# Reordering the written schedule of an attention stage: value tiles by halves of rows, normalisation next to its sums, pool weights loaded early

## The chip, the cores and the metric

The kernel runs on one core of a Trainium2 chip. The metric is device time in microseconds (us) of one execution; the median of several runs is compared. Each run of a comparison is made on the same chip as the kernel it is compared with.

## The reference: what is computed

One layer of an encoder trunk over 1024 tokens of width 1024, all in float32:

```python
hn = rmsnorm(h, norm_mix_g[i])
z = hn @ w_in[i]                       # 512 pool columns, then q, k, v of 8 heads x 64
a = pool_mixer(u, pool_w[i], ...)      # 4 groups, trailing windows 2, 4, 8, 16
o = chunk_attention(q, k, v, rel_bias[i])  # chunk of 64 attends to itself and 8 chunks before
h = h + jnp.concatenate([a, o], axis=-1) @ w_out[i]
# then a gated MLP with a causal convolution and GELU, a sigmoid gate with a
# per-layer input, and a last rmsnorm
```

The softmax is over the band of 576 positions with a relative-position bias for each head. The change touches the attention stage and the first half of the output projection behind it; the MLP and the gate, which take the last 830 us or so, stay as they are.

## The kernel before

**Products.** Every float32 product is made of three matmuls: each operand is split into a high part (rounded, written by ScalarE with a copy) and a low part (the rest, written by VectorE with a subtraction). The helper `mm3` (lines 117 to 119) issues high x high, high x low and low x high into one PSUM bank. `split` (lines 122 and 123) makes the two parts.

**The attention stage** works on pairs of heads (4 pairs) and, inside a pair, on tiles of 128 queries (8 tiles). A *unit* is one pair and one query tile; tiles 0 and 1 share a unit, so there are 7 units in a pair (`PER`) and 28 in all (`NU`). `unit(u)` writes the instructions of a unit in this order:

1. `probs_t(u - 1)`: TensorE transposes the probabilities of the unit before (line 407) into PSUM banks 2 and 3, and what has no room there into banks 6 and 7. `probs_out` brings them to SBUF as high part (ScalarE, line 426) and low part (VectorE, line 427).
2. `scores(u)`: TensorE makes the scores of the unit (line 383) in banks 4 to 7.
3. `softmax`: VectorE adds the bias and takes the extreme of each row (lines 351 and 355), ScalarE takes the exponential and its sum (line 363), VectorE takes the reciprocal (line 365), and the rows are scaled by it: those of the first head of the pair by VectorE (line 361), those of the second by ScalarE (line 359).
4. *Fill*: TensorE works on the projection of what later units need: q and k of the next pairs, the second half of the values, then the pool columns. The generators `project` and `project_v` yield after each step: one block of 128 rows of the contraction (three matmuls of 512 columns) in `project`, two blocks (six matmuls of 256 columns) in `project_v`. A unit is allowed a number of steps (`ROOM`, 5.5 to 7), and a running `credit` carries over what was taken too much or too little.
5. `values(u - 1)`: after every second query tile, TensorE multiplies values and probabilities (lines 451 and 452). Before it, while the unit is not the last and the state variable `at[0]` is below 1.6, more fill steps are taken, and each is charged to `credit`. `at[0]` says how far the current accumulation has come: it keeps the product away from the first moments of an accumulation, since it uses the PSUM bank that the projection is not in.

The projections alternate between PSUM banks 0 and 1 (`bankn`). A finished half is read out of its bank by `qk_out` (VectorE, line 263), by `v_outs` (ScalarE 254, VectorE 255) or for the pool columns by line 549. `lay` makes the high and low parts of q and k (lines 292 to 296). Weights are split by `split_later` (lines 475 and 472) into one of two ring slots (`wring`); the two row halves of the value weights (`wv2[0]`, `wv2[1]`) lie in the same two slots.

**The order** on TensorE, ScalarE and VectorE in this stage is written out, not planned: TensorE takes its instructions as the program issues them, and for the other two `push(due, ...)` files each instruction under a due time inside its unit, and `flush()` issues what is filed in the order of these due times. So the numbers in `push` set the order on both engines. Waits between engines follow from what is read and written; two engines are never let into the same PSUM bank at once, and the later one in program order waits. Outside this stage a planner orders all engines but TensorE, and it may bring later instructions into idle places of the stage.

**Behind the stage** come the pool mixer and the output projection. `tail` holds the running sums of the two narrow pool groups (VectorE, lines 564 to 580), which use a piece of the buffer `F` from 57.5 KB on as scratch; the two wide groups run on GpSimd (`later`). `out_mm(d, ...)` accumulates one block of output rows (12 matmuls), and `mix(g)` between them multiplies one pool group by its weights in banks 6 and 7 and reads it out with line 594. The pool weights are loaded and split in the first call of `mix`, into ring slot 1, which the last projection of the stage uses until its end.

Of the kernel before, what the change touches and what calls it, by code (L numbers as in the profile page):

```python
# [11 lines left out]
P = 128  # L12
# [70 lines left out]
def trunk(tc, xT, pT, vecs, w_qk0, w_in, w_v, bias, counts, pool_w, w_out, w_up, w_down,  # L83
# [4 lines left out]
    with tc.tile_pool(name="sb", bufs=1) as sb, \  # L88
# [20 lines left out]
        def f(kb, n):  # L109
            return F[:, int(kb * KW):int(kb * KW) + n]  # L110

        def rv(ap):
            return ap.bitcast(F32)

        def mm3(ps, ahi, alo, bhi, blo, first, last, more=False):

            pe.matmul(ps, ahi, bhi, start=first, stop=False, skip_group_check=more)  # L117
            pe.matmul(ps, ahi, blo, start=False, stop=False, skip_group_check=more)  # L118
            pe.matmul(ps, alo, bhi, start=False, stop=last, skip_group_check=more)  # L119

        def split(src, hi, lo, pinned=False):
            both = (act.activation(hi, src, AF.Copy),  # L122
                    dve.tensor_tensor(lo, src, rv(hi), ALU.subtract))  # L123
            if pinned:
                for i in both:
                    tc.keep_in_program_order(i)
# [122 lines left out]
        def v_outs(t, half, ps):  # L249
            s = rstd_tok[:, t:t + 1]  # L250
            pv = ps.rearrange("p (h c) -> p h c", h=4)
            hs = slice(4 * half, 4 * half + 4)
            hi, lo = V[:, t, hs, 0:HD], V[:, t, hs, HD:2 * HD]
            return (lambda: act.activation(hi, pv, AF.Copy, scale=s),
                    lambda: dve.scalar_tensor_tensor(lo, pv, s, rv(hi), ALU.mult, ALU.subtract))
# [5 lines left out]
        def qk_out(c, h, ps):  # L261
            hs = slice(h * 512, (h + 1) * 512)
            dve.tensor_tensor(qk32[c][:, hs], ps, rstd_bc[:, hs], ALU.mult)
# [4 lines left out]
        def push(t, *fns):  # L268

            for n, fn in enumerate(fns):  # L270
                pending.append((t + 0.8 * n, len(pending), fn))

        def flush():
            todo = sorted(pending, key=lambda p: p[:2])
            pending.clear()
            owed.clear()
            for _, _, fn in todo:
                fn()
# [65 lines left out]
        def softmax(todo):  # L344

            for i, (x, b, ps, S, s_) in enumerate(todo):
                z = 2 * i / len(todo)

                def least(b=b, ps=ps, S=S, s_=s_):
                    if len(ps.shape) == 3:  # L350
                        dve.tensor_tensor_reduce(  # L351
                            S.rearrange("p (a b) -> p a b", a=2), ps,
                            b.rearrange("p (a b) -> p a b", a=2), 1.0, BIG, ALU.add, ALU.min, s_[:, 0:1])
                    else:
                        dve.tensor_tensor_reduce(S, ps, b, 1.0, BIG, ALU.add, ALU.min, s_[:, 0:1])

                def scaled(x=x, S=S, s_=s_):
                    if x:
                        act.activation(S, S, AF.Copy, scale=s_[:, 2:3])  # L359
                    else:  # L360
                        dve.tensor_scalar(S, S, s_[:, 2:3], None, ALU.mult)
                push(1.0 + 0.8 * z, least)
                push(1.9 + 0.85 * z, lambda S=S, s_=s_: act.activation(  # L363
                    S, S, AF.Exp, bias=s_[:, 0:1], scale=-1.0, accum_out=s_[:, 1:2]))
                push(3.4 + 0.35 * z, lambda s_=s_: dve.reciprocal(s_[:, 2:3], s_[:, 1:2]))
                push(3.9 + 0.1 * z, scaled)

        halves = [slice(HD * x, HD * x + HD) for x in range(2)]

# [51 lines left out]
        def probs_out(todo):  # L421
            n = 0
            for x, q, a, b, bank, ps in todo:
                src = ps.rearrange("p a (k q) -> p a k q", q=HD)
                hi, lo = [PT[x][:, y, a:b, q:q + P].rearrange("p k (a q) -> p a k q", a=2) for y in range(2)]
                push(0.9 if bank > 3 else 0.3 * n, lambda hi=hi, src=src: act.activation(hi, src, AF.Copy))  # L426
                push(2.6 + 0.3 * n, lambda lo=lo, src=src, hi=hi: dve.tensor_tensor(lo, src, rv(hi), ALU.subtract))  # L427
                n += bank < 4

        credit, turns = 0.0, []  # L430
# [35 lines left out]

        def split_later(ct, parts, soon=False):

            t = now[0] if soon else max(5.2, now[0] + 0.4)
            for i, (src, hi, lo) in enumerate(parts):  # L470
                def low(src=src, hi=hi, lo=lo, end=i == len(parts) - 1):
                    dve.tensor_tensor(lo, src, rv(hi), ALU.subtract)
                    if end:
                        there.add(ct)
                push(t + 0.7 * i, lambda src=src, hi=hi: act.activation(hi, src, AF.Copy), low)

        def v_weights(z):
            split_later(("v", z), [(wvr[z][:, k], wv2[z][0][:, k], wv2[z][1][:, k])
# [38 lines left out]
        def project_v():  # L517
            v_weights(1)
            flush()
            for t in range(NTOK):  # L520
                bankn[0] += 1
                bank = bankn[0] % 2
                if bank in owed:
                    flush()
                for k in range(KT):
                    if (t, k) == (NTOK - 1, 4):
                        weights(8 + 3)
                    mm3(PS[:, bank, 0:256], XTH[t // 4][:, k, t % 4 * P:(t % 4 + 1) * P],
                        XTL[t // 4][:, k, t % 4 * P:(t % 4 + 1) * P], wv2[k // 4][0][:, k % 4], wv2[k // 4][1][:, k % 4],
                        k == 0, k == KT - 1)  # L530
                    if k % 2:
                        at[0] = 0.36 * (k + 1)
                        yield True
                push(now[0] + 0.2, *v_outs(t, 1, PS[:, bank, 0:256]))
                owed.add(bank)
                v_ready.append(t)

        def project_qk(p):

            for x in (1, 0):  # L540
                def evac(h, ps, x=x):
                    push(now[0] + 0.2, lambda: qk_out(x, h, ps))
                    qk_ready.append((p, x, h))
                yield from project(4 + 4 * x + p, evac, (p - 1, (x,)))

# [34 lines left out]
                eng.scalar_tensor_tensor(u[:, f0:n], src[:, f0:n], 1.0 / win, u[:, f0:n], ALU.mult, ALU.subtract)  # L580

        def mix(g):
            if g == 2:
                t = load(pool_w, 512)
                split(t, pwh, pwl)
            yh, yl = ya[g % 2]
            a32 = a32s[g % 2]
            split(U[:, g, HIST:], yh, yl)
            for h in range(2):
                hs = slice(h * 512, (h + 1) * 512)  # L590
                ps = PS[:, 6 + h]
                gs = slice(g * P, (g + 1) * P)
                mm3(ps, pwh[:, gs], pwl[:, gs], yh[:, hs], yl[:, hs], True, True)
                act.activation(a32[:, hs], ps, AF.Identity, bias=pbs[:, g:g + 1],
                               scale=vec[:, C_PS + g:C_PS + g + 1])
                split(a32[:, hs], catp[h][:, g, 0], catp[h][:, g, 1])
# [39 lines left out]
        def lay_due(u):  # L636

            for c, x, h in list(qk_ready):
                if u >= (c - 1) * PER + (0 if x else PER - 1 if h else 2):
                    qk_ready.remove((c, x, h))  # L640
                    push(max(5.2, now[0] + 0.4), *lay(c, x, h))

        for h in range(3):
            load_bias(h)()
# [39 lines left out]

        weights(8 + 1)
        flush()
        with tc.manual_schedule(engines={mybir.EngineType.Activation, mybir.EngineType.DVE}):
            for u in range(NU + 1):
                unit(u)
        for _ in fill:  # L690
            flush()
        flush()
        run_later(len(later))
        for fn in tail:
            fn()
# [59 lines left out]
        first_b = (2, 3, 4, 5, 0, 1, 6, 7)  # L755
        for z, d in enumerate(first_d):
            out_mm(d, 0, first_b[z], attn, True, False)
            if 1 <= z <= 4:
                mix((2, 3, 0, 1)[z - 1])
        for d in first_d:  # L760
            sp.dma_start(H[d], xT[d])
        out_weights(1, pooled)
# [670 lines left out]
```

## Time and profile before

| what | us |
|---|---|
| median of 3 runs | 1139.28 (1137.82 to 1139.57) |
| the profiled execution | 1138.94, span 1137.2 |
| TensorE busy | 1119.2 (98% of the span) |
| VectorE, ScalarE, GpSimd busy | 863.7, 588.7, 144.3 |
| mean granted TensorE clock | 0.996 of full speed |
| attention stage | from about 54 to 271 us |
| output projection, first half | from about 282 to 338 us |

Times in the profile count from the first instruction. A matmul's end is modelled, so starts are more reliable than durations. A group line shows an instruction's source line, engine, operation, what it writes and reads, the shapes, the count, busy time and mean, then the idle time of the engine just before and who ended it. A list of waits says who waited for whom, how long in total, how often, and the longest. A timeline row shows start, duration and instruction, and in brackets the idle time before it.

### The profile page before, as it was taken

Reading aid. Unit: us, or ns where it says so; the run is one execution under the profiler, and the core shown is the slowest. Engines: PE = TensorE matmul, PEld = TensorE weight load, DVE = VectorE, ACT = ScalarE, POOL = GpSimd, SP = SyncE. Lnnn points to the kernel's source line nnn. Section 1 sums busy time; section 2 is a strip of 40 time slices with the busy share of each in tenths; the row PEclk is TensorE's granted clock in tenths of the full one; section 3 lists DMA queues with packets and bytes.
Section 4 is the critical chain, followed back from the end, with each engine's and each line's share of the span. In section 5 each row is a group of like instructions: output and inputs, shape, how many; then the busy total and the mean of one; then the engine's idle time right before and its main releaser. Section 6 shows DMA issues by size and latency. Waiting matters only on the chain.

```text
span 1137.2 us, 16199 instructions
## 1 busy us (share of the span) xinstructions
PE 1119.2 (98%) x5914; PEld 936.4 (82%) x5914; DVE 863.7 (76%) x1508; ACT 588.7 (52%) x1052; POOL 144.3 (13%) x188
## 2 busy tenths in 40 slices
PE   9999999999999999999999999999999999999997
PEld 7988787888788888888888887888888888888887
DVE  8577657678758888887787878777878789986845
ACT  8376667665654554444444444444444445564634
POOL 0000000065002200120112011211021102000000
PEclk9999999999999999999999999999999999999999
DMA  7111101105500154575557655765576555520003
GB/s 279 38 37 43 38 24 37 50 23 183 194 13 16 48 150 146 135 178 142 132 155 158 164 133 150 157 162 142 149 153 157 153 149 115 164 93 19 1 30 118
DMA packets 64879, 125.91 MB, mean 111 GB/s; under 512 B 7328, under 2 KB 8736, under 8 KB 64800
## 3 DMA queue, kind: packets, MB, share of 16 engines
q1 hardware_dynamic: 50688, 99.38, 26.8%
q0 software_dynamic: 13824, 25.17, 14.0%
q8 instruction: 46, 0.75, 0.3%
q10 hardware_dynamic: 288, 0.33, 0.1%
q14 instruction: 33, 0.27, 0.1%
HBM read 110.18 MB, written 14.68 MB: 110 GB/s over the span
## 4 chain that ended last, share of the span: by engine, by line
PE 88%; DVE 6%; ACT 3%; issue 2%; DMA 1%; POOL 0%; SPq 0%; POOLq 0%; DVEq 0%; ACTq 0%
PE PS L117 28%; PE PS L118 27%; PE PS L119 27%; DVE B L427 2%; DVE F L351 2%; PE PS L451 1%; PE PS L452 1%; ACT B L426 1%; PE PS L383 1%; PE PS L407 1%; ACT F L454 1%; DVE R L123 0%; PE PS L739 0%; DMA F<-in_xT 0%; ACT F L359 0%
## 5 line engine op out<-in xcount | busy, mean ns | idle before, releaser
L117 PE MATMUL PS<-R 128*128 128x512 f32 (+1 forms) x1104 | 425.6, 386 | 1.7 <-ACT F L909 0.8
L118 PE MATMUL PS<-R 128*128 128x512 f32 (+1 forms) x1104 | 422.4, 383 | 0.2 <-DVE R L228 0.2
L119 PE MATMUL PS<-R 128*128 128x512 f32 (+1 forms) x1104 | 421.9, 382 | 0.0
L117 PEld LDWEIGHTS PS<-R 128*128 128x128 f32 x1104 | 208.2, 189 | 45.1 <-issue 2.1
L118 PEld LDWEIGHTS PS<-R 128*128 128x128 f32 x1104 | 208.2, 189 | 40.2 <-DVE R L228 1.5
L119 PEld LDWEIGHTS PS<-R 128*128 128x128 f32 x1104 | 207.9, 188 | 40.5
L122 ACT ACTIVATE R<-F 128x512 fp32r<-128x512 f32 (+2 forms) x221 | 138.1, 638 | 175.2 <-PE PS L118 80.2
L123 DVE TENSOR_TENSOR R<-F,R 128x512 fp32r<-128x512 f32 (+2 forms) x221 | 152.8, 703 | 37.3 <-ACT R L122 35.9
L822 DVE TENSOR_TENSOR F<-F 128x512 f32<-128x512 f32 x88 | 61.5, 699 | 49.0 <-DMA F<-in_w_up 45.7
L1132 DVE TENSOR_TENSOR F<-F,PS 128x512 f32<-128x512 f32 x140 | 92.3, 680 | 6.2 <-PE PS L119 6.0
L122 ACT ACTIVATE BQ<-RW 128x512 fp32r<-128x512 f32 x90 | 52.6, 622 | 77.1 <-PE PS L118 73.1
L1075 POOL DMA_DIRECT2D RW<-Yd x56 | 49.4, 883 | 262.6 <-DMA RW<-Yd 201.0
L1075 POOL DMA_DIRECT2D RW<-in_w_down x40 | 36.1, 946 | 233.8 <-DMA RW<-in_w_down 193.0
L123 DVE TENSOR_TENSOR BQ<-RW,BQ 128x512 fp32r<-128x512 f32 x90 | 59.0, 683 | 2.1 <-PE PS L118 1.3
L118 PE MATMUL PS<-BQ 128*128 128x512 f32 x140 | 54.6, 390 | 0.1
L119 PE MATMUL PS<-BQ 128*128 128x512 f32 x140 | 54.5, 389 | 0.0
L118 PE MATMUL PS<-R,BQ 128*128 128x512 f32 x140 | 54.5, 389 | 0.0
L117 PE MATMUL PS<-BQ 128*128 128x512 f32 x140 | 54.5, 389 | 0.0
L117 PE MATMUL PS<-R,BQ 128*128 128x512 f32 x140 | 54.5, 389 | 0.0
L119 PE MATMUL PS<-R,BQ 128*128 128x512 f32 x140 | 54.5, 389 | 0.0
L958 ACT ACTIVATE F<-F,vec 128x1024 f32<-128x1024 f32 (+1 forms) x25 | 28.6, 1143 | 48.6 <-DVE F L933 42.9
L363 ACT ACTIVATE F<-F,small 128x640 f32<-128x640 f32 (+4 forms) x64 | 44.0, 691 | 16.7 <-DVE small L351 15.0
(179 smaller groups left out, 1704.6 us busy)
## 6 DMA issues: line engine op xcount, KB each, us to landing
F<-in_w_up SPq DMA_DIRECT2D x91, 256.0 KB, 4.3
RW<-Yd SPq DMA_DIRECT2D x60, 256.0 KB, 3.6
RW<-Yd POOLq DMA_DIRECT2D x56, 256.0 KB, 5.0
RW<-in_w_down SPq DMA_DIRECT2D x50, 256.0 KB, 2.8
RW<-in_w_down POOLq DMA_DIRECT2D x40, 256.0 KB, 6.3
Yd<-F SPq DMA_DIRECT2D x40, 256.0 KB, 3.8
F<-in_w_in SPq DMA_DIRECT2D x10, 512.0 KB, 3.5
F<-in_xT SPq DMA_DIRECT2D x16, 256.0 KB, 5.8
```

The source lines that it names most:

```text
L117: pe.matmul(ps, ahi, bhi, start=first, stop=False, skip_group_check=more)
L118: pe.matmul(ps, ahi, blo, start=False, stop=False, skip_group_check=more)
L119: pe.matmul(ps, alo, bhi, start=False, stop=last, skip_group_check=more)
L122: both = (act.activation(hi, src, AF.Copy), dve.tensor_tensor(lo, src, rv(hi), ALU.subtract))
L123: dve.tensor_tensor(lo, src, rv(hi), ALU.subtract))
L351: dve.tensor_tensor_reduce(S.rearrange("p (a b) -> p a b", a=2), ps, b.rearrange("p (a b) -> p a b", a=2), 1.0, BIG, ALU.add, ALU.min, s_[ ...
L363: push(1.9 + 0.85 * z, lambda S=S, s_=s_: act.activation(S, S, AF.Exp, bias=s_[:, 0:1], scale=-1.0, accum_out=s_[:, 1:2]))
L427: push(2.6 + 0.3 * n, lambda lo=lo, src=src, hi=hi: dve.tensor_tensor(lo, src, rv(hi), ALU.subtract))
L822: return dve.tensor_tensor(rawu[to], rawu[a], rawu[b], op)
L958: act.activation(y, Gb[:, 2 + a:2 + b], AF.Identity, bias=vec[:, C_CB + fi:C_CB + fi + 1], scale=cw(2))
L1075: pool.dma_start(t, src, accum_op=ALU.add)
L1132: dve.tensor_tensor(t, t, PS[:, 4 + d], ALU.subtract if n in (1, 5) else ALU.add)
```

## The change

Five things change, all in the order of work.

- **Softmax order.** The reciprocals are due earlier (2.95 and 3.5 instead of 3.4 and 3.75), and the scaling on VectorE is due right behind its reciprocal (3.0 instead of 3.9). The copy of the transposed probabilities out of banks 6 and 7 is due at 3.6 instead of 0.9; the subtractions for all pieces but the first are due at 3.55 to 4.4 instead of 2.9 to 3.5.
- **Reading out.** `qk_out` and `v_outs` are due 0.2 earlier, the second instruction of `v_outs` 0.5 instead of 0.8 after the first; `lay` is due from 4.8 instead of 5.2.
- **Value tiles.** For the first two tiles (0 and 1) and the last two (6 and 7) the first four row blocks of both tiles are done first, then the last four of both, so two accumulations are open at once. While such a pair is open `at[0]` is 0.0, and it rises to 0.72 and 1.44 in the last half of the second tile. The split of the second half of the value weights is due before the rest (`now - 0.3`). The weights of the next projection are asked for before the second half of tile 6 instead of in the middle of tile 7.
- **Pool weights** are loaded in unit 23 into the buffer `F` at 57.5 KB, and split right behind the stage, ahead of `tail`.
- **The mixer** starts after the third block of the output projection instead of the second.

```diff
-                push(3.4 + 0.35 * z, lambda s_=s_: dve.reciprocal(s_[:, 2:3], s_[:, 1:2]))
-                push(3.9 + 0.1 * z, scaled)
+                push(2.95 + 0.55 * z, lambda s_=s_: dve.reciprocal(s_[:, 2:3], s_[:, 1:2]))
+                push(3.9 + 0.1 * z if x else 3.0 + 0.55 * z, scaled)
...
-                push(0.9 if bank > 3 else 0.3 * n, lambda hi=hi, src=src: act.activation(hi, src, AF.Copy))
-                push(2.6 + 0.3 * n, lambda lo=lo, src=src, hi=hi: dve.tensor_tensor(lo, src, rv(hi), ALU.subtract))
+                push(3.6 if bank > 3 else 0.3 * n, lambda hi=hi, src=src: act.activation(hi, src, AF.Copy))
+                push(4.4 if bank > 3 else 3.55 + 0.05 * n if n else 2.6, lambda lo=lo, src=src, hi=hi: dve.tensor_tensor(lo, src, rv(hi), ALU.subtract))
...
-            t = now[0] if soon else max(5.2, now[0] + 0.4)
+            t = now[0] - 0.3 if soon else max(5.2, now[0] + 0.4)
...
-                push(t + 0.7 * i, lambda src=src, hi=hi: act.activation(hi, src, AF.Copy), low)
+                push(t + 0.7 * i * (not soon), lambda src=src, hi=hi: act.activation(hi, src, AF.Copy))
+                push(t + (0.25 + 0.02 * i if soon else 0.8 + 0.7 * i), low)
...
-            for t in range(NTOK):
-                bankn[0] += 1
-                bank = bankn[0] % 2
-                if bank in owed:
-                    flush()
-                for k in range(KT):
-                    if (t, k) == (NTOK - 1, 4):
-                        weights(8 + 3)
...
+            order = [(t, z) for t in range(NTOK) for z in range(2)]
+            order[1:3] = order[2:0:-1]
+            order[-3:-1] = order[-2:-4:-1]
+            banks = {}
+            for t, z in order:
+                if z == 0:
+                    bankn[0] += 1
+                    banks[t] = bankn[0] % 2
+                    if banks[t] in owed:
+                        flush()
+                ps = PS[:, banks[t], 0:256]
+                paired = t in (0, 1, NTOK - 2, NTOK - 1)
+                if (t, z) == (NTOK - 2, 1):
+                    weights(8 + 3)
+                for k in range(4 * z, 4 * z + 4):
...
                     if k % 2:
-                        at[0] = 0.36 * (k + 1)
+                        at[0] = 0.36 * (k + 1) if not paired else 0.36 * (k - 3) if z and t % 2 else 0.0
                         yield True
-                push(now[0] + 0.2, *v_outs(t, 1, PS[:, bank, 0:256]))
-                owed.add(bank)
-                v_ready.append(t)
+                if z:
+                    hi, lo = v_outs(t, 1, ps)
+                    push(now[0], hi)
+                    push(now[0] + 0.5, lo)
+                    owed.add(banks[t])
+                    v_ready.append(t)
...
-                    push(now[0] + 0.2, lambda: qk_out(x, h, ps))
+                    push(now[0], lambda: qk_out(x, h, ps))
...
-            if g == 2:
-                t = load(pool_w, 512)
-                split(t, pwh, pwl)
...
-                    push(max(5.2, now[0] + 0.4), *lay(c, x, h))
+                    push(max(4.8, now[0] + 0.4), *lay(c, x, h))
...
+        pw = f(57.5, 512)
         with tc.manual_schedule(engines={mybir.EngineType.Activation, mybir.EngineType.DVE}):
             for u in range(NU + 1):
                 unit(u)
+                if u == NU - PER + 2:
+                    sp.dma_start(pw, pool_w)
         for _ in fill:
             flush()
         flush()
+        split(pw, pwh, pwl)
...
-            if 1 <= z <= 4:
-                mix((2, 3, 0, 1)[z - 1])
+            if 2 <= z <= 5:
+                mix((2, 3, 0, 1)[z - 2])
```

More of the change, by code (lines that the diff above doesn't have):

```diff
@@ L519, in project_v @@
             flush()
-            for t in range(NTOK):
-                bankn[0] += 1
-                bank = bankn[0] % 2
-                if bank in owed:
-                    flush()
-                for k in range(KT):
-                    if (t, k) == (NTOK - 1, 4):
-                        weights(8 + 3)
-                    mm3(PS[:, bank, 0:256], XTH[t // 4][:, k, t % 4 * P:(t % 4 + 1) * P],
-                        XTL[t // 4][:, k, t % 4 * P:(t % 4 + 1) * P], wv2[k // 4][0][:, k % 4], wv2[k // 4][1][:, k % 4],
+            order = [(t, z) for t in range(NTOK) for z in range(2)]
[13 more added lines that the diff above has]
+                for k in range(4 * z, 4 * z + 4):
+                    mm3(ps, XTH[t // 4][:, k, t % 4 * P:(t % 4 + 1) * P],
+                        XTL[t // 4][:, k, t % 4 * P:(t % 4 + 1) * P], wv2[z][0][:, k % 4], wv2[z][1][:, k % 4],
                         k == 0, k == KT - 1)
                     if k % 2:
-                        at[0] = 0.36 * (k + 1)
+                        at[0] = 0.36 * (k + 1) if not paired else 0.36 * (k - 3) if z and t % 2 else 0.0
                         yield True
-                push(now[0] + 0.2, *v_outs(t, 1, PS[:, bank, 0:256]))
-                owed.add(bank)
-                v_ready.append(t)
+                if z:
[4 more added lines that the diff above has]
+                    v_ready.append(t)
         def project_qk(p):
```

## The prediction

> **What bounds the kernel now.** I read the page's busy times first, then stretches of the span, then TensorE's waits inside the stage that the change reorders.
>
> ```profile
> PE 1119.2 (98%) x5914; PEld 936.4 (82%) x5914; DVE 863.7 (76%) x1508; ACT 588.7 (52%) x1052; POOL 144.3 (13%) x188
> ...
> 54.00:310.50 256.50, 248.13 (x1876) 209.58 (x1875) 184.53 (x464) 168.80 (x369) 36.13 (x60) 0.99 0.22 70
> 130.20:139.98 9.78, 7.37 (x42) 6.67 (x42) 5.98 (x14) 4.46 (x10) 0.00 (x0) 0.83 0.16 54
> ...
> 132.01:135.43 3.42, 1.36 (x7) 0.96 (x7) 3.42 (x9) 2.25 (x6) 0.00 (x0) 1.00 0.00 0
> 135.43:138.84 3.41, 3.20 (x15) 3.20 (x16) 1.16 (x4) 1.30 (x2) 0.00 (x0) 0.50 0.47 154
> ...
> PE PS L407 <- DVE F L361: 2.7, 5, 0.9
> PE PS L118 <- DVE B L472: 1.3, 2, 0.8
> PE PS L117 <- ACT B L122: 1.1, 1, 1.1
> PE PS L117 <- ACT B L475: 1.1, 1, 1.1
> PE PS L451 <- DVE F L263: 0.7, 2, 0.6
> PE PS L117 <- DVE R L255: 0.7, 2, 0.4
> PE PS L451 <- DVE R L255: 0.3, 1, 0.3
> PE PS L383 <- DVE R L296: 0.2, 1, 0.2
> ```
>
> The first row says that TensorE is the bound (98%), and the change neither adds nor removes a matmul: only waits and clock can move. The rows behind it give TensorE's share of each stretch: 248.13 of 256.50 us from 54 to 310.5, so about 8.4 us of idle time, which is what the waits below it add up to. The start of the second half of the values (130.20 to 139.98) is the worst place: 42 matmuls in 9.78 us, with the granted clock at 0.50 for 3.41 us. All the change can win is these 8.4 us and the slow clock; the question is what it puts in their place.
>
> **The change part by part.**
>
> *Softmax order.* Unit 27 shows the chain that holds the transposes (line 407) in five units.
>
> ```profile
> 257.07 0.31 PE L383 MATMUL PS<-R 64*128 64x320 f32 x2
> ...
> 260.39 0.39 PE L118 MATMUL PS<-R 128*128 128x512 f32 x1
> 260.62 0.39 PE L119 MATMUL PS<-R 128*128 128x512 f32 x1
> 261.72 0.67 PE L407 MATMUL PS<-ident,F 64*128 64x64 f32 x14 [0.72 <-DVE F L361]
> ...
> 257.90 0.82 DVE L351 CUSTOM_DVE_ANT_0 F<-PS,F 128x640 f32<-128x640 f32 x1 [0.52 <-ACT B L426]
> ...
> 258.65 0.82 DVE L351 CUSTOM_DVE_ANT_0 F<-PS,F 128x640 f32<-128x640 f32 x1
> ...
> 259.39 1.61 DVE L427 TENSOR_TENSOR B<-PS,B 128x640 fp32r<-128x640 f32 x3
> ...
> 261.11 0.56 DVE L361 TENSOR_SCALAR F<-F,small 128x640 f32<-128x640 f32 x1
> ```
>
> The scores end at 257.38, but VectorE starts only at 257.90, behind ScalarE's copy out of banks 6 and 7 (0.52). With that copy due at 3.6 VectorE starts at 257.42: 0.75 and 0.74 for the extremes, 0.74 for the first of the three subtractions, 0.15 reciprocal, 0.5 scaling: the first head is scaled near 260.4 instead of 261.67. What is late next is the second subtraction (about 0.6 with its reciprocal): it frees bank 2, into which the transposes go, at 261.05. TensorE is free at about 261.0, so 0.05 of the 0.72 is left. In the same way two others (0.55, 0.17) go, and 0.89 becomes 0.4, since a read-out of values lies between. In the unit that waited 0.39 (512 wide, no piece in banks 6 and 7) nothing is won ahead and the subtraction now comes last: 0.55. Together 2.7 becomes 1.0: **-1.7**.
>
> *Reading out and lay earlier.* The waits for lines 263, 296 and two of the three for line 255 (0.7, 0.2 and 0.7) go, as these instructions move ahead of one or two VectorE instructions: **-1.7**. The subtractions they pass are needed only 12 matmuls into the product of values.
>
> *First value tiles.*
>
> ```profile
> 130.43 0.28 PE L118 MATMUL PS<-R 128*128 128x256 f32 x1
> ...
> 131.63 0.28 PE L119 MATMUL PS<-R 128*128 128x256 f32 x1
> 132.98 0.38 PE L117 MATMUL PS<-B,R 128*128 128x256 f32 x1 [1.07 <-ACT B L475]
> ...
> 129.66 0.43 DVE L457 TENSOR_TENSOR F<-PS,F 64x256 f32<-64x256 f32 x1
> ...
> 132.11 0.69 DVE L263 TENSOR_TENSOR F<-PS,F 128x512 f32<-128x512 f32 x1
> ...
> 133.45 0.68 DVE L472 TENSOR_TENSOR B<-F,B 128x512 fp32r<-128x512 f32 x1
> ...
> 139.98 0.84 PE L407 MATMUL PS<-ident,F 64*128 64x64 f32 x20
> ```
>
> Matmuls of 256 columns start 0.12 apart (130.43 to 131.63, ten steps), so 42 of them are 5.0 us; the stretch took 9.78. In the new order the first half of tile 1 follows at 131.65 and needs no new weights, but it does need its bank: tile 1 takes the bank of the last q projection, and its read-out (line 263) is now due at 1.93, behind both weight subtractions (1.88, 1.90) and both extremes. VectorE: free at 130.1, extremes 1.5, weight subtractions 1.2, read-out 0.69: 133.55. So TensorE waits 1.9 us there, and nothing afterwards, since the weights are ready at 132.9. New length 5.0 + 1.9 = 6.9 against 9.78: **-2.9**, the slow clock included: its 15 matmuls in 3.41 us are worth 1.8 us at 0.12, so it cost 1.6.
>
> *Last value tiles.* Here the change costs. While tiles 6 and 7 are open `at[0]` never reaches 1.6 (0.0, then 0.72 and 1.44). In unit 14 the product of values comes up just as tile 6 has begun, so its loop now runs to the third block of the next projection: 10 steps more instead of 2. That puts 10 value blocks (30 matmuls, 3.6 us) and 3 blocks of 512 columns (9 times 0.23, 2.1 us) into unit 14, 5.6 us, and `credit` falls to -9.5 instead of -1.5: unit 15 gets no fill and unit 16 two steps instead of seven.
>
> ```profile
> 158.29 0.95 PE L383 MATMUL PS<-R 64*128 64x256 f32 x12
> ...
> 164.43 0.48 DVE L255 SCALAR_TENSOR_TENSOR R<-PS,small,R 128x256 fp32r<-128x256 f32 x1 [0.69 <-ACT R L254]
> ...
> 168.43 0.77 PE L383 MATMUL PS<-R 64*128 64x384 f32 x6
> ...
> 172.67 0.38 PE L451 MATMUL PS<-B,R 128*128 128x256 f32 x1 [0.34 <-DVE R L255]
> ...
> 179.43 0.74 PE L407 MATMUL PS<-ident,F 64*128 64x64 f32 x16
> ...
> 170.80 0.81 DVE L427 TENSOR_TENSOR B<-PS,B 128x128 fp32r<-128x128 f32 x3
> ...
> 171.05 0.60 ACT L363 ACTIVATE F<-F,small 128x384 f32<-128x384 f32 x1
> ```
>
> Moved work costs nothing only if what it covered is short. In unit 15 scores end at 169.2. The four subtractions (170.80 to 172.01) now follow both reciprocals, and the second waits for the exponential that ends at 171.65 and its sum: subtractions from 171.95 to 173.05. The product, which the fill let start at 172.67, can start at 172.4 and waits 0.2 inside: 3.2 us of idle TensorE where there was fill, and only 0.25 us won. Unit 16 has 1.4 us of fill against a chain of about 3.4 us behind its scores: some 2 us idle, and about 0.9 us sooner than before (179.43). New, too: the first half of tile 7 needs tile 5's bank, 1.4 us after tile 5 has ended; its read-out is last in the unit (before, it ended at 164.91, 5.7 us behind the scores, which ended at 159.24; tile 5 takes 2.9 of that and half a tile 1.4): 1.4 us wait; the old wait for tile 6's bank is among those gone above. Sum 5.6 + 1.4 - 0.25 - 0.9: **+5.9**.
>
> *The clock there.* The clock fell to 0.50 at 135.43, behind 3.42 us in which 7 matmuls ran (0.8 us of work at 0.12 each): about 2.6 idle us were enough. The new 3.2 us in unit 15 are more, so I take one more drop, at 1.2 us (the old one cost 1.6, and part of this one falls into waits): **+1.2**; its bounds are 0 and two drops, 3. The Trainium skill, "TensorE: Matmul & The Clock Gate", Part 1, says that the clock is halved only after a window of about 3.4 us without work, and that these windows run free of the kernel; by its letter 3.2 us would not do, and the sum would be 1.2 lower. The trace's own drop, in a window with 7 matmuls, speaks against the letter, and for a drop that depends on where the window falls.
>
> *Pool weights and mixer.*
>
> ```profile
> 287.87 0.63 ACT L122 ACTIVATE B<-F 128x512 fp32r<-128x512 f32 x1 [3.42 <-DMA F<-in_pool_w]
> ...
> 288.55 0.50 PE L117 MATMUL PS<-B 128*128 128x512 f32 x1 [1.08 <-ACT B L122]
> ...
> 290.38 1.43 ACT L594 ACTIVATE F<-PS,small,vec 128x512 f32<-128x512 f32 x2
> ...
> 269.50 0.98 DVE L564 TENSOR_TENSOR F<-F 128x271 f32<-128x271 f32 x1
> ...
> 276.18 0.44 DVE L564 TENSOR_TENSOR F<-F 128x271 f32<-128x271 f32 x1
> ```
>
> The transfer moves to unit 23 on the SyncE queue; its buffer was last read in unit 20, so it holds up nothing behind it there, and the output weights no longer queue behind it: the 1.08 goes. The last `mix` now stands right ahead of the block that uses bank 6; line 594 (0.77 for one) against 0.69 of matmuls between: 0.3 back, up to 1.2 where ScalarE is late. And `tail`, whose scratch lies where the pool weights land, can start only behind their split, which waits for the last projection (about 282), instead of at 269.50: some 3 us of VectorE work (seven pieces, the first 0.98, the later ones near 0.44) move behind 282. The mixer's later place covers it: it gives groups 0 and 1 1.6 us more, and the two wide groups' subtractions (1.2 each) can move ahead. **-0.8**, between -1.1 and +3.
>
> **Sum:** -1.7 - 1.7 - 2.9 + 5.9 + 1.2 - 0.8 = 0.0 against the profiled 1138.94 us, which stands 0.3 below the median: 1139.0.
>
> **The rivals.**
>
> *Faster: the chain in units 15 and 16 is shorter and the clock stays up.* These units lose the value read-outs and weight splits that VectorE had there (lines 255 and 472). No drop gives 1137.8; if the two waits, 5.2 us by my chain, are also 1 to 3 us shorter, 1135 to 1136.7. It decides if the product of unit 15 starts less than 2 us behind its scores. For it: the row of 170.80 is close behind the scores. Against: two exponentials of 0.6 in a row stand ahead of the last subtractions.
>
> *Slower: `tail` behind the pool weights.* If the planner keeps the wide groups' subtractions behind the split, all 3 us of VectorE work and line 594's 1.2 come onto TensorE's path: 1139 - 0.3 + 4 = 1143. It decides if group 0's subtraction ends later than TensorE's fourth block. For it: VectorE is busy nearly without a break in this stretch before. Against: 1 to 1.5 us of slack at each `mix`.
>
> *The pairing does what it says:* no wait for a bank at tile 1 or 7 would give 3.3 us more, 1135.7; only the due times of the two read-outs speak on that, against it.
>
> **How the numbers follow.** About 0.2% (2.3 us) is what a measurement of this kernel tells from no change. No change within it: 0.46. Faster (the first and third rival): 0.27. Slower (the second, or two drops): 0.27. The likeliest case alone reaches from 1137 to 1141; with both sides the range is 1135.4 to 1143.
>
> **What would show it.** In the new profile: no wait on line 361 above 0.6; at the first value tiles one wait for line 263 near 1.9 in place of three; one for line 255 near 1.4 in unit 14; then a wait of some 3 us at line 451 and one near 2 at line 407 two units on; the clock at 0.50 once; no wait for pool weights. I am wrong if the loop in unit 14 doesn't take the extra steps, or if waits turn up behind 282.

## The result and the profile after

The changed kernel takes 1140.51 us (median of 12 runs, 1138.46 to 1142.21); the kernel before takes 1138.76 us beside it (12 runs, 1137.62 to 1140.56). The ratio is 1.0016, 95% interval 1.0008 to 1.0025: slower by 1.8 us, where no change (1139.0) was predicted. The time lies inside the predicted range, and 1.8 us is less than the 2.3 us that the prediction counted as no change; but the interval leaves no change out, so the change did move the time, and not as forecast.

The profiled execution of the changed kernel took 1138.46 us (span 1136.7); its mean granted clock is 0.998, that of the other eleven, which are 1.6 to 3.7 us longer, 0.994 to 0.997, so this trace shows the waits of a usual run but not its clock.

Stretches of the span, with the columns of the prediction's rows (start, end and length, busy time and count of TensorE, its weight loads, VectorE, ScalarE and GpSimd, granted clock, share of DMA, GB/s):

```profile
54.00:310.50 256.50, 245.40 (x1874) 207.77 (x1874) 187.28 (x464) 169.58 (x369) 35.40 (x60) 1.00 0.22 70
169.99:173.40 3.41, 1.03 (x11) 0.54 (x7) 2.82 (x11) 3.18 (x10) 0.00 (x0) 1.00 0.00 0
172.21:175.63 3.42, 1.85 (x25) 1.72 (x27) 1.91 (x9) 2.27 (x7) 0.00 (x0) 1.00 0.00 0
```

TensorE is idle for 11.1 us of this stretch (256.50 - 245.40), 2.7 more than before, and its clock is full throughout, even behind the stretch from 169.99, in which it was busy for 1.03 us (the third row is taken up in the last section). TensorE's waits in the same stretch:

```profile
PE PS L407 <- DVE B L427: 2.8, 4, 1.8
PE PS L452 <- DVE B L427: 2.0, 1, 2.0
PE PS L117 <- DVE F L263: 1.7, 1, 1.7
PE PS L117 <- ACT B L122: 1.6, 1, 1.6
PE PS L117 <- DVE R L255: 1.2, 1, 1.2
PE PS L118 <- DVE B L123: 0.8, 1, 0.8
PE PS L451 <- ACT B L426: 0.8, 1, 0.8
PE PS L117 <- ACT F L602: 0.2, 1, 0.2
```

Every wait for line 361 is gone, and so are those for the weight splits of lines 475 and 472. In their place stand one at the first value tiles (L263), one at the last (L255), three behind the unit that lost its fill (L426, L427), three short ones at the transposes (0.98 us of line 427's 2.8), and three behind the stage. Where they lie, from the timeline (line 575 is the 564 of before, 602 the 594, 776 the load of the GELU table):

```profile
132.62 0.38 PE L117 MATMUL PS<-R 128*128 128x256 f32 x1 [1.67 <-DVE F L263]
...
160.05 0.39 PE L117 MATMUL PS<-R 128*128 128x256 f32 x1 [1.19 <-DVE R L255]
...
171.41 0.35 PE L451 MATMUL PS<-B,R 128*128 128x256 f32 x1 [0.75 <-ACT B L426]
173.78 0.38 PE L452 MATMUL PS<-B,R 128*128 128x256 f32 x1 [2.01 <-DVE B L427]
...
179.61 0.28 PE L407 MATMUL PS<-ident,F 64*128 64x64 f32 x2 [1.82 <-DVE B L427]
...
280.02 0.69 DVE L123 TENSOR_TENSOR B<-F,B 128x512 fp32r<-128x512 f32 x1 [0.50 <-PE PS L118]
...
281.23 0.43 DVE L575 TENSOR_TENSOR F<-F 128x271 f32<-128x271 f32 x1
...
297.00 0.41 DVE L591 SCALAR_TENSOR_TENSOR F<-F 128x252 f32<-128x252 f32 x1
...
297.26 1.28 ACT L776 ACT_TABLE_LOAD   x1
...
298.67 1.43 ACT L602 ACTIVATE F<-PS,small,vec 128x512 f32<-128x512 f32 x2
...
301.03 1.05 ACT L122 ACTIVATE B<-F 128x1024 fp32r<-128x1024 f32 x1
...
302.13 0.49 PE L117 MATMUL PS<-B 128*128 128x512 f32 x1 [1.60 <-ACT B L122]
...
303.39 0.50 PE L118 MATMUL PS<-B 128*128 128x512 f32 x1 [0.77 <-DVE B L123]
```

The first five waits are those that the prediction foretold (1.9; 1.4; 3.2, which came in two pieces, 2.76 in all; 2.0). The last two, 2.4 us, were not in the forecast. They are read backwards: TensorE needs the two halves of pool group 1; ScalarE makes the high half at 301.03, behind a table load and two read-outs; the running sums that the half is made of ended only at about 297.5, because the running sums began at 281.23, right behind the split of the pool weights (280.02), instead of at 269.50.

### The profile page after: what moved, and what is told of

Its sections match the earlier page's. It is cut to its first block, busy times and chain, and to the rows that moved or that the text cites. A ratio compares the mean times of both kernels' runs of the same rounds, so it can differ in the third digit from the quotient of the medians.

```text
span 1136.7 us, 16213 instructions
## 1 busy us (share of the span) xinstructions
PE 1116.6 (98%) x5914; PEld 934.5 (82%) x5914; DVE 866.1 (76%) x1508; ACT 589.0 (52%) x1052; POOL 144.2 (13%) x188
## 4 chain that ended last, share of the span: by engine, by line
PE 92%; DVE 3%; ACT 2%; issue 2%; DMA 1%; SPq 0%; POOL 0%; POOLq 0%; DVEq 0%; ACTq 0%
PE PS L117 29%; PE PS L118 28%; PE PS L119 28%; PE PS L383 2%; PE PS L452 2%; PE PS L451 2%; PE PS L407 2%; DVE F L351 1%; ACT R L122 1%; DMA F<-in_w_qk 1%; DVE B L427 0%; ACT F L602 0%; PE PS L751 0%; DVE F L361 0%; DMA F<-in_w_out 0%
```

## The experiments

All differences in us below are a run's ratio to the kernel before, which ran on the same chip beside it, times 1138.8.

| kernel | median us | ratio [95% interval] | us against before |
|---|---|---|---|
| the change | 1140.51 | 1.0016 [1.0008, 1.0025] | +1.8 |
| e1: change, other scratch | 1140.71 | 1.0021 [1.0010, 1.0032] | +2.4 |
| e2: change without the last pair | 1134.42 | 0.9957 [0.9941, 0.9973] | -4.9 |
| e3: e2 + e1 | 1135.74 | 0.9972 [0.9962, 0.9983] | -3.2 |
| e4: e3 + later weight split | 1134.58 | 0.9959 [0.9943, 0.9975] | -4.7 |
| e5: e2 + mixer at its old place | 1135.12 | 0.9964 [0.9952, 0.9977] | -4.1 |
| e6: e3 + mixer at its old place | 1131.36 | 0.9940 [0.9926, 0.9953] | -6.8 |
| e7: e2 + all behind the stage as before | 1131.97 | 0.9943 [0.9930, 0.9955] | -6.5 |
| e8: e4 + mixer at its old place | 1129.94 | 0.9930 [0.9917, 0.9943] | -8.0 |
| e9: change, all behind the stage as before | 1138.43 | 0.9997 [0.9987, 1.0008] | -0.3 |
| e10: before + softmax order | 1132.81 | 0.9944 [0.9931, 0.9957] | -6.4 |
| e11: before + first value tiles | 1137.13 | 0.9986 [0.9977, 0.9996] | -1.6 |

The intervals are 1 to 1.8 us to either side; for the difference of two rows that makes about 1.5 to 2.5 us (an estimate from the intervals), and smaller differences are not told apart.

**e1: the running sums' scratch elsewhere.** The buffer `F` at 57.5 KB, where the pool weights now land, was the scratch of `tail`; here `tail` gets another place.

```diff
-        temps = [[f(57.5, 272), f(58.5625, 272)], [T1, T2]]
+        temps = [[f(17, 272), f(19.5, 272)], [T1, T2]]
```

> The changed kernel with the scratch of the two narrow pool groups moved from 57.5 KB (where the pool weights now land) to the buffers of the scores, which are free by then; nothing else. Theory A (the scratch makes the running sums wait for the split of the pool weights, and that puts 1.60 + 0.77 us of waits on TensorE at the last mixer block): the running sums start near 267 again, these two waits go, a wait of about 0.2 for bank 6 stays; 2.0 to 2.4 us below the changed kernel, so 0.2 to 0.6 us below the kernel before. Theory B (these waits come from the mixer's later place): they stay, and the time is that of the changed kernel, 1.0016 of before.

The time did not move (+2.4 us against +1.8, within the intervals). From the timeline of e1:

```profile
268.86 0.98 DVE L575 TENSOR_TENSOR F<-F 128x271 f32<-128x271 f32 x1
...
293.71 0.63 ACT L122 ACTIVATE R<-F 128x512 fp32r<-128x512 f32 x1 [1.84 <-DMA F<-in_w_out]
...
304.94 1.28 ACT L776 ACT_TABLE_LOAD   x1
306.34 1.43 ACT L602 ACTIVATE F<-PS,small,vec 128x512 f32<-128x512 f32 x2
```

The sums start at 268.86 again, and the waits of 1.60 and 0.77 are gone: that the scratch held the sums up is shown. But TensorE now waits elsewhere, as its list of waits says:

```profile
PE PS L117 <- ACT F L602: 3.7, 2, 2.2
```

ScalarE reads bank 6 out late twice: once because it stands at a weight split that waits for its transfer (293.71), and once because the table load is ordered ahead of the last two read-outs (304.94). The gain that the scratch alone should have brought did not come: lifting one cause exposed the next.

**e2: the last pair of value tiles in the old order.**

```diff
-            order[-3:-1] = order[-2:-4:-1]
...
-                paired = t in (0, 1, NTOK - 2, NTOK - 1)
-                if (t, z) == (NTOK - 2, 1):
+                paired = t in (0, 1)
+                if (t, z) == (NTOK - 1, 1):
```

> The changed kernel with the last two value tiles one after the other again, the weights of the next projection asked for in the middle of tile 7; the first two tiles stay paired. Theory A (the pairing at the end moves 5.6 us of fill out of units 15 and 16 and adds a wait for a bank): the waits of 1.19, 0.75, 2.01 and 1.82 us go, one of about 0.3 comes back, the clock no longer drops there: 5.5 to 7.5 us below the changed kernel, ratio to before 0.995 to 0.997. Theory B (the moved fill is only shifted and the loss sits behind the stage): not more than 1 us below the changed kernel.

The median falls by 6.1 us (6.7 by the ratios). Of the waits between 159 and 180, one of 0.47 is left. The longest that remain, beside that at the first value tiles, are the pair of waits behind the stage, here from e2's list:

```profile
PE PS L117 <- ACT B L122: 1.8, 1, 1.8
...
PE PS L118 <- DVE B L123: 0.8, 1, 0.8
```

So the paired last tiles cost what the prediction said they would, and the rest of the change is worth 4.9 us although it still has the waits behind the stage.

**e3 and e4: both, and the read-out of the last q projection ahead of the weight split.** e3 joins e1 and e2. e4 also delays the split of the second value weights on VectorE, so that line 263 goes ahead of it:

```diff
-                push(t + (0.25 + 0.02 * i if soon else 0.8 + 0.7 * i), low)
+                push(t + (0.35 + 0.02 * i if soon else 0.8 + 0.7 * i), low)
```

> Both edits together: the scratch moved and the last two value tiles one after the other. If the two losses are separate, as I hold, their gains add: 7.5 to 9.5 us below the changed kernel, ratio to before 0.9935 to 0.995. If the earlier arrival behind the stage eats the second, less than 6.

> As e3_both, and the subtractions of the second half of the value weights due 0.1 later, so that the read-out of the last q projection stands ahead of them on VectorE. Theory A (tile 1 waits for that read-out): the wait of 1.67 us becomes 0.5 to 0.7, and the second halves do not wait: 1.0 to 1.2 us below e3_both. Theory B (the wait is for the weights): no change, or the wait moves to the second half of tile 0.

e3 came out no faster than e2 (0.9972 against 0.9957), where its expectation had the two gains add, with the waits of e1 behind the stage (0.72 and 2.23 us for line 601, the 602 of the change). In e4 the wait at the first value tiles falls from 1.68 to 0.47: tile 1 waits for that read-out, not for the weights. The median falls by 1.2 us, as expected; by the intervals alone that could be nothing.

**e5 and e6: the mixer at its old place.** e5 does this to e2, e6 to e3:

```diff
-            if 2 <= z <= 5:
-                mix((2, 3, 0, 1)[z - 2])
+            if 1 <= z <= 4:
+                mix((2, 3, 0, 1)[z - 1])
```

> As e2_lastpair (last value tiles one after the other, scratch still where the pool weights land), with the mixer starting after the second block again. Theory A (running sums held back by the shared scratch): the mixer asks for its last group 2.7 us sooner and the sums are no earlier, so the wait of 2.5 us in e2_lastpair grows to 4 to 5: 2 to 3 us above e2_lastpair. Theory B (the later place is the cause): the waits go and it is 2 to 2.5 us below e2_lastpair.

> As e3_both (last value tiles one after the other, scratch moved), with the mixer starting after the second block again. Theory C, after e1_scratch and e3_both (two causes, each enough: the shared scratch holds the running sums, and the later place lets the planner put ScalarE's table load and weight splits ahead of line 602 while TensorE needs bank 6 at once): all waits from 280 to 310 us go but for 0.5 at most; 2.5 to 3 us below e3_both and 2 to 2.5 below e2_lastpair. Theory B2 (an earlier arrival behind the stage meets late transfers of the output weights): 2 us or more of waits stay there.

e5 is like e2 (0.9964); neither of its theories, 2 us or more slower or faster, had that. The sums are late as before, and TensorE waits 1.26 and 0.76 us for the two halves of group 1; the table load still stands ahead of the last two read-outs, but no matmul waits for these. e6 is 2.7 to 3.6 us faster than either part alone. From its timeline, and from its list of waits:

```profile
296.31 0.79 ACT L601 ACTIVATE F<-PS,small,vec 128x512 f32<-128x512 f32 x1
297.11 1.28 ACT L775 ACT_TABLE_LOAD   x1
```

```profile
PE PS L117 <- ACT F L601: 0.4, 1, 0.4
```

With both undone the table load comes after all read-outs and one wait of 0.4 us is left. With only one undone it stands ahead of the last two (e1, e3, e5), in the change ahead of the last four. So the lateness behind the stage has two causes, each enough by itself: the shared scratch, which makes the sums late (e5), and the mixer's later place, in which TensorE needs bank 6 at once while ScalarE reads it out behind a weight split or the table load (e1, e3). How much of this is the table load's was not tested alone, and why the planner's costs bring it forward was not looked into.

**e7 and e9: all behind the stage as before.** Pool weights loaded in the first call of `mix`, mixer behind the second to fifth block; e7 does this to e2, e9 to the change itself.

```diff
         def mix(g):
+            if g == 2:
+                t = load(pool_w, 512)
+                split(t, pwh, pwl)
...
-        pw = f(57.5, 512)
...
-                if u == NU - PER + 2:
-                    sp.dma_start(pw, pool_w)
...
-        split(pw, pwh, pwl)
...
-            if 2 <= z <= 5:
-                mix((2, 3, 0, 1)[z - 2])
+            if 1 <= z <= 4:
+                mix((2, 3, 0, 1)[z - 1])
```

> As e2_lastpair, with everything behind the stage as in the kernel before: the pool weights loaded in the mixer, the mixer after the second block. Only the order inside the stage and the first pair are left of the change. One wait of about 1.1 us for the pool weights: 1.2 to 1.6 us below e2_lastpair, about 5.5 to 7 us below the kernel before. It prices what the change does behind the stage: the difference to e2_lastpair.

> The changed kernel with only its last two parts undone: the pool weights loaded and split in the first call of mix again, and the mixer after the second to fifth block; the paired last value tiles stay. Theory C (the sign came from what the change does behind the stage, 2.45 us by e2 and e7): about 1138.1, ratio 0.9985 to 1.0005, with the waits of 1.67, 1.19, 0.75, 2.01 and 1.82 in the stage unchanged and one wait near 0.9 behind it. Theory D (e7's gain belongs to the unpaired tiles, since what is brought forward out of the tail depends on the stage in front of it): 1139.5 to 1141, ratio above 1.001.

e7 is 1.6 us faster than e2 by the ratios (2.4 by the medians), which the intervals alone do not tell apart; e9 is 2.2 us faster than the change (2.1 by the medians), which they do. e9's waits, from its list, are those of the change inside the stage, and behind it only the old one for the pool weights:

```profile
PE PS L407 <- DVE B L427: 2.4, 4, 1.4
PE PS L452 <- DVE B L427: 2.0, 1, 2.0
...
PE PS L117 <- ACT B L122: 1.0, 1, 1.0
```

This is the direct test of the sign: with only these two of the five edits undone the kernel is as fast as before (0.9997, interval 0.9987 to 1.0008), which is what the prediction said of the whole.

**e8: the best of these.** e4 with the mixer at its old place.

> As e6_place_scratch, with the read-out of the last q projection ahead of the value weights' subtractions as in e4_readout: 1.0 to 1.2 us below e6_place_scratch (the wait of 1.67 us becomes 0.5), 7.5 to 9 us below the kernel before.

1129.94 us, 0.9930 of the kernel before [0.9917, 0.9943]: it beats both kernels, before and changed. Its 1.2 us on e6 is within the intervals, but the wait at the first value tiles falls from 1.67 to 0.47 again. TensorE's waits of over 0.1 us between 54 and 345 us add up to 2.4 us, none above 0.47.

**e10 and e11: one part alone on the kernel before.** e10 has the softmax order only, e11 the first value tiles by halves with the earlier split of their weights.

```diff
-                push(3.4 + 0.35 * z, lambda s_=s_: dve.reciprocal(s_[:, 2:3], s_[:, 1:2]))
-                push(3.9 + 0.1 * z, scaled)
+                push(2.95 + 0.55 * z, lambda s_=s_: dve.reciprocal(s_[:, 2:3], s_[:, 1:2]))
+                push(3.9 + 0.1 * z if x else 3.0 + 0.55 * z, scaled)
...
-                push(0.9 if bank > 3 else 0.3 * n, ...)
-                push(2.6 + 0.3 * n, ...)
+                push(3.6 if bank > 3 else 0.3 * n, ...)
+                push(4.4 if bank > 3 else 3.55 + 0.05 * n if n else 2.6, ...)
```

> The kernel before with the softmax order alone (reciprocals, scaling, copy out of banks 6 and 7, later subtractions). The prediction's step by itself: waits for line 361 fall from 2.7 in all to about 1.0, in place of them short waits at line 407, nothing else moves: -1.7, ratio 0.9985. Rival: the later subtractions hold up the read-outs queued behind them, whose due times are the old ones here, so waits at lines 117 and 118 grow by 0.5 to 1.5: ratio 0.999 to 1.0005.

> The kernel before with the first two value tiles by halves alone, with the earlier split of the second half of the value weights. The prediction's step: three waits and the slow clock at the first tiles go, one wait near 1.7 for line 263 (0.2 more here, where that read-out is due 0.2 later) comes: -2.9, ratio 0.9975. Rival: the waits only move to a later unit, since the fill taken in unit 10 is the same: ratio 0.999 to 1.0.

e10 gives -6.4 us where either theory had at most 1.7. Stretches of e10, its longer waits, and three rows of its VectorE:

```profile
54.00:310.50 256.50, 252.23 (x1904) 213.53 (x1903) 188.34 (x466) 169.95 (x372) 35.63 (x60) 1.00 0.22 70
...
130.87:134.29 3.42, 1.72 (x10) 1.30 (x10) 3.38 (x8) 2.46 (x7) 0.00 (x0) 1.00 0.00 0
```

```profile
PE PS L118 <- DVE B L472: 1.1, 2, 0.8
PE PS L117 <- ACT B L122: 1.0, 1, 1.0
PE PS L407 <- DVE B L427: 0.8, 2, 0.5
PE PS L117 <- ACT B L475: 0.6, 1, 0.6
...
```

```profile
129.13 0.82 DVE L351 CUSTOM_DVE_ANT_0 F<-PS,F 128x640 f32<-128x640 f32 x1
...
130.62 0.69 DVE L263 TENSOR_TENSOR F<-PS,F 128x512 f32<-128x512 f32 x1
...
131.95 0.68 DVE L472 TENSOR_TENSOR B<-F,B 128x512 fp32r<-128x512 f32 x1
```

Idle time falls from 8.4 to 4.3 us, and in this execution the slow clock is gone: 4.1 and 1.6 us of the 6.4. VectorE no longer stands behind the copy out of banks 6 and 7 when the scores are done. In the kernel before it did so twelve times between 54 and 271 us, ten of them for 0.5 to 1.1 us, a wait that e10's list does not have:

```profile
DVE F L351 <- ACT B L426: 12.3, 12, 4.1
```

So everything filed behind the extremes runs earlier, also what the edit doesn't touch: at the first value tiles line 263 starts at 130.62 instead of 132.11 and the weight subtraction at 131.95 instead of 133.45. Of these 1.5 us, 1.0 is that TensorE comes there sooner, too (its scores start at 127.97 instead of 128.97). No run moves the copy without the reciprocals and subtractions, so what each is worth is not shown. The waits there shrink from 2.4 to 1.7 us (1.1 + 0.6), and in the emptiest 3.42 us there TensorE is busy for 1.72 us instead of 1.36, and no drop of the clock follows in this execution.

e11 gives -1.6. Its stretches and its wait at the first tiles:

```profile
131.36:134.77 3.41, 1.25 (x10) 1.25 (x11) 3.41 (x8) 1.34 (x4) 0.00 (x0) 1.00 0.14 32
134.77:138.19 3.42, 3.42 (x18) 3.42 (x18) 0.89 (x4) 0.96 (x2) 0.00 (x0) 0.50 0.31 121
```

```profile
PE PS L117 <- DVE F L263: 2.2, 1, 2.2
```

Three waits became one of 2.2 us, and in this execution the slow clock stayed. By the traces e11 has only 0.2 us less idle time than the kernel before (8.17 instead of 8.37), so most of its 1.6 us must be clock or chance. Its other runs speak for clock: in all thirteen profiled executions of this case a mean clock of 0.998 or more goes with no drop ahead of the last 6 us, one of 0.997 or less with a drop; six of e11's ten runs have 0.998, and five of the 23 of the kernel before beside it.

## Why the prediction was wrong

From the kernel before to e10, e7, e9 and the change one group of edits is added at a time, so the measured steps add up to the whole (each is uncertain by 1 to 2 us, and another order would share them out differently: the first value tiles alone give -1.6 in e11):

| step of the prediction | predicted | measured |
|---|---|---|
| softmax order | -1.7 | -6.4 (e10) |
| reading out, first value tiles | -1.7 - 2.9 | -0.1 (e7 less e10) |
| last value tiles, clock there | +5.9 + 1.2 | +6.2 (e9 less e7) |
| pool weights and mixer | -0.8 | +2.2 (change less e9) |
| sum | 0.0 | +1.8 |

**The step that failed is "The mixer's later place covers it".** The first two rows agree in sum (-6.3 against -6.5) and the third is 0.9 too high; the last is 3.0 off and turns the sign. Its mechanism was half seen: `tail` did start only behind the split of the pool weights (281.23 against 269.50), the wide groups' subtractions did move ahead (276.44 and 278.30), the wait of 1.08 did go, and 0.17 did come at line 602 where 0.3 was given. But the later place does not cover the lateness of group 1. In the kernel before, its sums end at 294.48, its high half is written at 297.11, and TensorE asks for it at 301.17 without a wait:

```profile
294.33 0.15 DVE L575 TENSOR_TENSOR F<-F 128x4 f32<-128x4 f32 x1
...
297.11 1.06 ACT L122 ACTIVATE B<-F 128x1024 fp32r<-128x1024 f32 x1
...
301.17 0.39 PE L117 MATMUL PS<-B 128*128 128x512 f32 x1
...
302.50 1.46 ACT L594 ACTIVATE F<-PS,small,vec 128x512 f32<-128x512 f32 x2
...
305.02 1.28 ACT L764 ACT_TABLE_LOAD   x1
```

The output projection starts at 281.87 there and at 279.97 in the change; counted from this start, TensorE asks for group 1 1.3 us later (1.6 predicted), and it had 3.0 us of slack there. But the sums end 4.9 us later, where 3 us of work were counted, and the high half is ready 5.8 us later, since ScalarE's queue adds 0.9: a table load, two read-outs and two weight splits (297.26 to 301.03) stand ahead of it. In the kernel before, the table load stands behind the last read-out, and the prediction left it out of the count. 5.8 less 1.3 and 3.0 leaves 1.5 us; the wait measured 1.60. The prediction's own sign of being wrong, waits behind 282, came.

The waits behind the stage are 1.5 us longer in the change than in e9 (2.5 against 1.0); the rest of the 2.2 can be clock, which the term did not hold. In e2 these two waits are followed by a drop (at 298.67), and the median of the mean clocks is 0.995 in the change's runs and 0.996 in e9's; the one trace of the change shows no such drop. The second rival named the right place, `tail` behind the pool weights. But its premise did not come (the wide groups' subtractions did not stay behind the split), it looked at group 0, where no wait came, and it gave 4 us and, together with two drops of the clock, a chance of 0.27. The cost lies within the bounds that the term was given (-1.1 to +3), so it was the value chosen inside them that failed.

**Softmax order, reading out, first tiles: right in sum by luck, wrong in the split.** The first row has 4.7 us of gain too little and the second 4.5 too much, and the two errors happen to cancel. The waits that the prediction said would remain at the transposes, 1.0 us, are there (0.47, 0.30 and 0.21 us for line 427). But the three steps were costed one by one against the same old trace, and their gains are largely the same gain. The 0.5 to 0.7 us by which VectorE starts earlier in a unit removes most of the waits that the later read-outs, and then the pairing, were to remove: with the old due times only 0.6 us of waits for line 255 are left in e10, none for lines 263 and 296. At the first value tiles pairing exchanges 1.70 us of waits (e10) for one of 1.67 (the change; 1.9 predicted): nothing. And the slow clock, 1.6 us, was booked to the pairing. In the profiled executions e10 is without it and e11 has it, but by the mean clocks two of e10's four runs and six of e11's ten are without a drop (0.998); which edit removes it, and how often, stays open.

**Last value tiles: right.** The bank of tile 7, the missing fill in unit 15 and the short fill in unit 16 all came, at 1.19, 2.76 and 1.82 us for 1.4, 3.2 and 2.0. e2 and e9 price the edit at 6.2 to 6.7 us with the clock, 7.1 predicted. The third rival, that pairing simply removes its waits, is out. The first, that the chain in unit 15 is shorter, had the right sign with 0.6 us (4.6 instead of 5.2) of the 1 to 3 it needed.

**The clock there: right in kind.** One drop of the clock was predicted, with 0 to two as its bounds. The profiled execution of the change has none, that of e9, with the same waits, has one of 3.41 us, and that of e1 one of 6.83 us. From e9's stretches:

```profile
170.25:173.67 3.42, 0.83 (x7) 0.34 (x3) 3.03 (x11) 3.17 (x11) 0.00 (x0) 1.00 0.00 0
173.67:177.08 3.41, 3.25 (x27) 3.02 (x27) 1.16 (x5) 1.74 (x4) 0.00 (x0) 0.50 0.00 0
```

In e9 the next wait, at 180.60, is 0.4 us shorter than in the change (1.42 against 1.82), so a part of a drop is given back, as the prediction allowed. That the other eleven runs of the change lose their 1.6 to 3.7 us to such drops is what their mean clocks suggest; no trace of those runs shows the place.

## What to carry to other kernels

Price edits that start the same engine earlier as one term: taken singly against the old trace each seems to win the same wait. When blocks move on one engine, write out the queue of every engine that serves them, with what a planner may put in between (here sums that ended 4.9 us later instead of 3, and a table load of 1.28 us), and count slack on these queues and not on the bound engine. Fill that is taken earlier must be matched by name to the chain it used to cover: here 5.6 us of TensorE's fill taken one unit early came back as 4.6 us of idle time one and two units later, and the bank that two open tiles need took 1.2 more.

## What the runs showed of the hardware

The clock falls behind stretches in which TensorE still works, and not each time. It was halved behind 3.4 us in which TensorE was busy for 1.36 us (before), 1.25 (e11), 0.83 (e9) and 1.33 (e1). It stayed full behind the 3.42 us with 1.72 us busy in e10, and also in the profiled execution of the change, which has such a stretch with 1.03 us and the same waits as e9 within 0.4 us. From e1's and e2's stretches:

```profile
169.71:173.12 3.41, 1.33 (x19) 0.84 (x16) 2.53 (x9) 3.38 (x11) 0.00 (x0) 1.00 0.06 25
```

```profile
298.67:302.09 3.42, 3.42 (x10) 2.52 (x9) 0.59 (x2) 2.52 (x4) 0.00 (x0) 0.50 0.56 208
```

In e1 it was low for two such stretches in a row (173.12 to 179.95). In e2 it fell at 298.67, behind the two waits of 1.8 and 0.8 us, so a wait of 2.5 us behind the stage also cost clock, which the term for the mixer didn't hold. The Trainium skill, "TensorE: Matmul & The Clock Gate", Part 1, lets the windows of about 3.4 us run free of the kernel: the trace agrees, since the lengths of 3.41 and 3.42 us recur and like waits drop the clock in one execution and not in another. Where it asks for an idle window, the measurement differs: the windows ahead of these drops held 3 to 19 matmuls.

The traces also show where the windows lie. Each of them has a last drop in its last 6 us, and the drop in the stage lies a whole number of windows of 3.413 us ahead of it: 292.0 of them in the kernel before (135.43 and 1132.12), 281.0 in e9 (173.67 and 1132.81), 243.0 in e2 (298.67 and 1128.11). Counted back in such steps from the last drop of the change (1131.36), a window border falls at 172.21, in the middle of its idle stretch, and the emptier of the two windows beside it has 1.85 us of TensorE work (the third row of the stretches above): the execution without the drop met the same waits with its windows shifted. One limit on busy time is not shown: on these borders the clock fell behind 1.72 us (e5, 293.46 to 296.87) and stayed full behind 1.67 (e4, 295.82 to 299.24).
